# One level of Strassen's product for all projections of x in a hybrid encoder block

## The chip, the core and the metric

The kernel runs on one core of a Trainium2 chip. The metric is the device time of one execution in microseconds (us); the median of three runs counts. The core has five engines that run side by side: TensorE (PE in the profile; PEld is its weight load), VectorE (DVE), ScalarE (ACT), GpSimd (POOL) and SyncE (SP), whose queue issues most DMAs.

## The reference

All arrays are float32. One layer over 1024 tokens of 1024 channels:

```python
h = rmsnorm(x, norm_mix_g)                      # (1, 1024, 1024)
z = h @ w_in                                    # 1024 -> 4*512 + 3*512 + 8 + 512 + 3*1024 columns
(hq, hf, hi, hg, fq, fk, fv, ff, mq, gate_logits) = split(z)
y_a = hgrn2(hq, hf, hi, hg)                     # gated recurrence, 4 heads, 128x128 state
y_b = fox(fq, fk, fv, ff)                       # forgetting attention, 8 heads of 64, causal
y_c = memory(mq, rmsnorm(mem) @ mem_kv_w)       # cross attention into 256 tokens, 4 heads of 128
gates = sigmoid(gate_logits)                    # three gates per channel
merged = gates[0]*(y_a @ w_br_hgrn) + gates[1]*(y_b @ w_br_fox) + gates[2]*(y_c @ w_br_mem)
x = x + merged @ w_out
x = x + conv_glu(rmsnorm(x, norm_ffn_g))        # up to 2*2816, causal conv of width 3, gelu, down
```

The projection `h @ w_in` is the part that the change touches: the columns `hq, hf, hg, mq` and the gates are wanted channel-major (channels on partitions), `hi, fq, fk, fv` token-major, and `ff` gives eight forget logits per token.

## The kernel before

Float32 products are made from three passes: each operand is split into a high part of reduced precision (`h`, a cast on ACT or POOL) and the rest (`l`, a subtraction on DVE), and `mm3` (L109 to L111) issues h·h, h·l and l·h into one PSUM bank. `split` is at L115 (cast on ACT), L119 (on POOL) and L123 (subtraction). A block of the contraction is 128 channels; a bank holds 512 float32 columns. There are eight banks in four tags: `pp` (three), `lg` (two), `tr` (two) and `po` (one).

Start-up. x arrives as eight slices `xk` of 128 channels by 1024 tokens, memory as `mt`, its weights as `wkv`. The list `SEQ` orders the work by hand: memory keys and values (`kv_chunk`), and as slices of x land, their split into `uh`, `ul` (L269, L270), and two gate chunks (`gate_step`) are multiplied slice by slice. x is split unnormalized; the norm's factor per token (`rt`, from rows of x that are loaded a second time, and `rx`, the same spread over partitions by a DMA through DRAM) is applied to the products.

Projections of x. A channel-major chunk (`cm_chunk`) is 128 columns of the weight against 1024 tokens: 2 halves x 8 blocks x 3 matmuls of 512 columns. A token-major piece (`token_major`) is 256 weight columns for 8 blocks of tokens: 8 x 8 x 3 matmuls of 256 columns.

Mixers. `fox_values` (token-major fv and the forget logits) run first, then fox runs over four pairs of heads. `weave` interleaves the program of a mixer with that of fill: `fox_attn` with the next pair's `fox_proj` and gate chunks (`gates_early`, results stored to DRAM as `gd`), the last pair with HGRN2's values, `hgrn_mix` with the next head's `hgrn_prep`, `mem_attn` with `mem_prep` and gates. `ahead` gives the mixers a head start of 300 places in priority; within that, a scheduler orders each engine's instructions when the kernel is built. Outputs of HGRN2 and memory stay in SBUF (`ya`, `yc`), those of fox go through DRAM and are loaded back as `yb` while the memory mixer runs.

Merge. `gates` goes over 24 chunks (three branches of eight): branch product (`br_chunk`), gate, sum. One gate chunk is still made there, the others come from DRAM. Then the output product, and the feed-forward part, which already uses one level of Strassen's product: `unit` makes four blocks of output from seven products of 12 matmuls, on seven families of operand blocks kept in SBUF (B11, T1, T2, B22, T3, B21, T4), with sums of weight blocks made on DVE. At its start `second_norm` makes the norm from column sums (L1030) and `spread` (L288).

Of the kernel before, what the change touches and what calls it, by code (L numbers as in the profile page):

```python
# [8 lines left out]
F32 = mybir.dt.float32  # L9
# [5 lines left out]
P = 128  # L15
# [14 lines left out]
NGF = [0, 3, 1, 2, 0, 5, 2, 0]  # L30
NG = [1, 1, 0, 3, 0, 0, 0, 3]
NPRE = 2 + sum(NG) + sum(NGF)
FOX_STEPS, HGRN_STEPS, MEM_STEPS = 28, 24, 7
FOX_LATE, MEM_LATE = 0.2, 0.3
AHEAD = 300
SEQ = ("k0 k1 k2 k3 x0 x1 g0 x2 mr g1 k4 s0 s1 x3 s2 k5 x4 mn mk s3 k6 x5 s4 k7 mv x6 s5 x7 xn s6 s7").split()
# [29 lines left out]
def tile_block(ctx: ExitStack, tc: tile.TileContext, xT, memT, x_rows, mem_rows, vec, fbias, mats, hmask, w_cm, w_hi, w_fqk, w_fv,  # L66
# [5 lines left out]
    wp = tc.alloc_tile_pool(name="wp", bufs=2, side="left")  # L72
# [22 lines left out]

# [29 lines left out]
    def rstd_small(out, ss, n):  # L125
        w = ss.shape[1]
        V.tensor_scalar(out, ss, 1.0 / n, EPS, ALU.mult, ALU.add)
        G.tensor_tensor(out, out, mhalf[:, :w], ALU.pow)

    wsplit = [S, V]  # L130

    def raw_weights(src, n):
        raw = wp.tile([P, 4 * 264], F32, tag="raw", name="raw", bufs=2)
        SP.dma_start(raw[:, :n], src)
        return raw

    def weights(src, shape, raw=None, hl=None, parts=1):

        n = shape[0] * shape[1]
        if raw is None:  # L140
            raw = raw_weights(src, n)
        if hl is None:
            hl = [wp.tile([P, 4 * 264], F32R, tag=t, name=t, bufs=3) for t in ("wh", "wl")]
        for i in range(parts):
            sl = slice(i * n // parts, (i + 1) * n // parts)
            split(wsplit[0], hl[0][:, sl], hl[1][:, sl], raw[:, sl], wsplit[1])
        return [t[:, :n].rearrange("p (a b) -> p a b", a=shape[0]) for t in hl]

    def cm_chunk(src, nk, rh, rl, by_channel=False):


        wh, wl = weights(src, (nk, P))
        if by_channel:
            pss = [ps_proj(), ps_proj()]
            for k in range(nk):
                for n, ps in enumerate(pss):
                    sl = slice(n * HB, (n + 1) * HB)
                    mm3(ps, wh[:, k, :], wl[:, k, :], rh[k][:, sl], rl[k][:, sl], k == 0, k == nk - 1)
            yield from enumerate(pss)
            return  # L160
        for n in range(2):
            ps = ps_proj()
            sl = slice(n * HB, (n + 1) * HB)
            for k in range(nk):
                mm3(ps, wh[:, k, :], wl[:, k, :], rh[k][:, sl], rl[k][:, sl], k == 0, k == nk - 1)
            yield n, ps

# [3 lines left out]
    pu = tc.alloc_tile_pool(name="pu", bufs=1, side="left")  # L171

    def both_parts(name):

        t = [[pu.tile([P, T], F32R, tag=f"u{p}{k}", name=f"{name}{p}{k}") for p in "hl"] for k in range(KC)]
        return [a for a, _ in t], [b for _, b in t]

    uh, ul = both_parts("u")
    rx = pu.tile([P, T], F32, tag="rx", name="rx")
    rt = pu.tile([P, 8], F32, tag="rt", name="rt")  # L180

    kvd = tc.dram_tile([P, 2, T], F32, name="kvd")

    p0 = tc.alloc_tile_pool(name="p0", bufs=1, side="right", reuse_waits="tile")
    mt = p0.tile([P, KC, NM], F32, tag="mt", name="mt")
    xk = [p0.tile([P, T], F32, tag="xk", name=f"xk{k}", bufs=5) for k in range(KC)]
    def row_tile(name):
        return p0.tile([P, 2 * HB], F32, tag="wkv", name=name, bufs=6)  # L190

    wkv = [row_tile(f"wkv{q}") for q in range(4)]
    mem_row = [row_tile(f"mr{i}") for i in range(2)]
    wkv += [row_tile(f"wkv{q}") for q in range(4, 8)]
    x_row = [row_tile(f"xr{i}") for i in range(6)]
    x_row[2:2] = [p0.tile([P, T], F32, tag="xk", name=f"xr{i}", bufs=5) for i in (6, 7)]
    SP.dma_start(cv, vec)
    for q in range(4):
        w = 2 if q else 1
        for i in range(2 // w):  # L200
            sl, ws = slice(2 * q + i, 2 * q + i + w), slice(i * HB, (i + w) * HB)
            SP.dma_start(mt[:, sl, :], memT[:, sl, :])
            SP.dma_start(wkv[q][:, ws], w_mkv[q][:, ws])
    SP.dma_start(ones, mats[:, P:2 * P])
    rgw = []
    for what in SEQ:
        if what[0] == "x" and what != "xn":
            k = int(what[1])
            SP.dma_start(xk[k], xT[:, k, :])
        elif what == "mr":  # L210
            for i in range(2):
                SP.dma_start(mem_row[i], mem_rows[i])
        elif what[0] == "g":
            br, j = order[int(what[1])]
            rgw.append(raw_weights(w_cm[16 + 8 * br + j], KC * P))
        elif what in ("k4", "k5", "k6", "k7"):
            q = int(what[1])
            SP.dma_start(wkv[q], w_mkv[q])
    SP.dma_start(ident, mats[:, 0:P])
    for i in range(8):  # L220
        last_row = SP.dma_start(x_row[i], x_rows[i])
# [1177 lines left out]
```

## Time and profile before

| | |
|---|---|
| median of 3 runs | 1768.04 us (1767.48 to 1768.28) |
| span of the profiled execution, first to last instruction | 1765.2 us, so 2.8 us less than the median |
| PE busy | 1749.7 us (99%), 9153 matmul records |
| DVE, ACT, POOL busy | 1127.0, 742.8, 330.9 us |
| mean granted TensorE clock | 0.999 |
| DMA | 213.71 MB, mean 121 GB/s |

The profile is of one execution. A plain float32 matmul leaves two records, one of reduced precision leaves one. Matmuls are pipelined: a record's duration is longer than the distance to the next, so busy time counts their union. A row of a group has: line, engine, operation, output<-inputs, shapes and count, then busy time, mean ns of one, and the engine's idle time before them with what ended it. A row of a window has its start and end, its length, then busy time and count for PE, PEld, DVE, ACT and POOL, the granted clock, the DMA engines' share and GB/s. A row of the timeline has the start, the duration, engine, line, operation and tiles, and the idle time before. A row of the chain has the start, the duration and what ran.

### The profile page before, as it was taken

How to read it: one execution, taken by the hardware profiler on the slowest of the kernel's cores; microseconds unless marked ns; L12 is line 12 of the kernel's file. 1: busy time of each engine (PE TensorE's matmuls, PEld its weight loads, DVE VectorE, ACT ScalarE, POOL GpSimd, SP SyncE). 2: the span in 40 equal slices, each digit the busy share in tenths (PEclk: the TensorE clock that was granted, in tenths of full speed). 3: DMA queues.
4: the chain of work that ended last, by engine and by line, in shares of the span. 5: the costliest groups of instructions: out<-in, count | busy, mean ns of one | idle time of the engine just before them, and what ended most of it. 6: DMA issues, size and time to landing. Idle time of an engine off the chain costs nothing.

```text
span 1765.2 us, 24344 instructions
## 1 busy us (share of the span) xinstructions
PE 1749.7 (99%) x9153; PEld 1483.6 (84%) x9153; DVE 1127.0 (64%) x2065; ACT 742.8 (42%) x1237; POOL 330.9 (19%) x416
## 2 busy tenths in 40 slices
PE   8999999999999999999999999999999999999999
PEld 6999899889988888888888888788888888778887
DVE  6236665665567787734446665787777877775654
ACT  8345555554544354324522143643433443433332
POOL 0015233343224333323100000111111111100000
PEclk9999999999999999999999999999999999999999
DMA  9311121221111111130144442465544444394682
GB/s 365 142 61 65 63 74 49 101 76 52 61 63 37 42 43 37 52 128 19 66 143 132 143 180 83 133 186 160 147 141 151 125 126 143 132 380 148 221 289 84
DMA packets 77014, 213.71 MB, mean 121 GB/s; under 512 B 8912, under 2 KB 11736, under 8 KB 76768
## 3 DMA queue, kind: packets, MB, share of 16 engines
q1 hardware_dynamic: 62016, 159.19, 25.8%
q0 software_dynamic: 14880, 52.96, 10.5%
q8 instruction: 72, 1.18, 0.3%
q14 instruction: 46, 0.38, 0.1%
HBM read 174.07 MB, written 61.12 MB: 133 GB/s over the span
## 4 chain that ended last, share of the span: by engine, by line
PE 98%; DMA 1%; ACT 0%; SPq 0%; DVE 0%; issue 0%; DVEq 0%
PE pp L110 22%; PE pp L111 22%; PE pp L109 22%; PE lg L110 4%; PE lg L111 4%; PE lg L109 4%; PE tr L109 2%; PE tr L110 2%; PE tr L111 2%; PE lg L700 2%; PE po L567 1%; PE lg L526 1%; PE po L566 1%; PE lg L525 1%; PE po L111 1%; PE po L110 1%
## 5 line engine op out<-in xcount | busy, mean ns | idle before, releaser
L111 PE MATMUL pp<-uh,wl 128*128 128x512 f32 x608 | 243.6, 401 | 0.0
L110 PE MATMUL pp<-ul,wh 128*128 128x512 f32 x608 | 243.2, 400 | 0.0
L109 PE MATMUL pp<-uh,wh 128*128 128x512 f32 x608 | 241.7, 397 | 0.0
L110 PE MATMUL pp<-wl,uh 128*128 128x256 f32 (+1 forms) x512 | 145.0, 284 | 0.0
L111 PE MATMUL pp<-wh,ul 128*128 128x256 f32 (+1 forms) x512 | 144.5, 283 | 0.0
L109 PE MATMUL pp<-wh,uh 128*128 128x256 f32 (+1 forms) x512 | 143.7, 283 | 0.0
L115 ACT CAST wh<-raw 128x1024 fp32r<-128x1024 f32 (+2 forms) x80 | 73.0, 914 | 158.7 <-PE pp L110 124.9
L109 PEld LDWEIGHTS pp<-uh,wh 128*128 128x128 f32 x608 | 115.3, 190 | 23.3
L110 PEld LDWEIGHTS pp<-ul,wh 128*128 128x128 f32 x608 | 114.5, 188 | 22.9
L111 PEld LDWEIGHTS pp<-uh,wl 128*128 128x128 f32 x608 | 114.4, 188 | 22.5
L123 DVE TENSOR_TENSOR wl<-raw,wh 128x1024 fp32r<-128x1024 f32 (+2 forms) x87 | 93.8, 1080 | 34.1 <-ACT wh L115 23.8
L1078 POOL DMA_DIRECT2D rw<-in_w_up x44 | 24.2, 557 | 466.5 <-DVE wl L123 413.3
L115 ACT CAST wh<-s 128x512 fp32r<-128x512 f32 x85 | 51.9, 619 | 124.7 <-PE pp L110 64.7
L110 PEld LDWEIGHTS pp<-wl,uh 128*128 128x128 f32 x512 | 96.4, 188 | 0.8
L111 PEld LDWEIGHTS pp<-wh,ul 128*128 128x128 f32 x512 | 96.5, 189 | 0.6
L109 PEld LDWEIGHTS pp<-wh,uh 128*128 128x128 f32 x512 | 96.2, 189 | 0.8
L115 ACT CAST dwh<-wr 128x1024 fp32r<-128x1024 f32 (+1 forms) x42 | 41.1, 980 | 121.4 <-PE tr L110 41.7
L115 ACT CAST wh<-rw 128x512 fp32r<-128x512 f32 x65 | 40.1, 620 | 86.7 <-PE pp L110 46.7
L123 DVE TENSOR_TENSOR dwl<-wr,dwh 128x1024 fp32r<-128x1024 f32 (+1 forms) x42 | 47.6, 1132 | 35.5 <-ACT dwh L115 35.1
L681 POOL TENSOR_TENSOR X<-X,kt 128x256 f32<-128x256 f32 x48 | 48.3, 1012 | 110.2 <-ACT X L680 110.1
L543 POOL TENSOR_SCALAR pt<-pt,st 128x128 f32<-128x128 f32 (+3 forms) x64 | 57.0, 891 | 63.3 <-DVE st L542 51.4
L541 ACT ACTIVATE pt<-pt,st 128x128 f32<-128x128 f32 (+3 forms) x64 | 49.7, 777 | 33.9 <-DVE st L538 29.4
(422 smaller groups left out, 4797.3 us busy)
## 6 DMA issues: line engine op xcount, KB each, us to landing
rw<-in_w_up POOLq DMA_DIRECT2D x44, 512.0 KB, 4.6
raw<-in_w_cm SPq DMA_DIRECT2D x40, 512.0 KB, 3.5
sd<-in_w_dn POOLq DMA_DIRECT2D x30, 512.0 KB, 6.0
br<-yd SPq DMA_DIRECT2D x30, 512.0 KB, 5.0
gd<-gt SPq DMA_DIRECT2D x46, 256.0 KB, 2.0
gt<-gd SPq DMA_DIRECT2D x46, 256.0 KB, 2.7
yd<-fc SPq DMA_DIRECT2D x44, 256.0 KB, 2.6
wr<-sd SPq DMA_DIRECT2D x20, 512.0 KB, 4.7
```

The source lines that it names most:

```text
L109: PE.matmul(ps, lh, rh, start=first, stop=False, skip_group_check=more)
L110: PE.matmul(ps, lh, rl, start=False, stop=False, skip_group_check=more)
L111: PE.matmul(ps, ll, rh, start=False, stop=last, skip_group_check=more)
L115: S.copy(out, in_)
L123: return (sub or V).tensor_sub(l, src, h.bitcast(F32))
L525: PE.matmul(ps[:, :w], qa[i][:, tsl], kh[i][:, s0:s0 + w], start=True, stop=False)
L526: fox_sets[p][3] = PE.matmul(ps[:, :w], qa[i][:, tsl], kl[i][:, s0:s0 + w], start=False, stop=True)
L541: S.activation(pt[:, :ns], pt[:, :ns], AF.Exp, bias=st[:, 2:3], accum_out=st[:, 3:4])
L543: G.tensor_scalar(pt[:, :ns], pt[:, :ns], st[:, 3:4], 0.0, ALU.mult, ALU.add)
L681: G.tensor_mul(Xk, Xk, Kv[:, :, 0, :])
L700: PE.matmul(o[:, b * 64:(b + 1) * 64], X[:, b * P:(b + 1) * P], Xq[:, b * bpb:(b + 1) * bpb, :], start=True, stop=True)
L1078: late["raw"] = G.dma_start(raw[:, 2 * i:2 * i + 2, :], src[:, 2 * i:2 * i + 2, :])
```

## The change

All projections of x are made by one level of Strassen's product. With x in quarters (two halves of the channels by two halves of the tokens) and the weight in quarters, seven products of half size replace eight.

- Families. x is normalized first: squares are summed over the slices as they land (`x_square`), the factor comes from column sums, a power on POOL and `spread`; each quarter is then multiplied by gain and factor (`normed`), combined and split into seven families of 4 x 128 channels by 512 tokens, which stay in SBUF until the mixers end. The rows of x are not loaded, and no gate chunk is made at start-up. The forget logits come from 16 plain float32 matmuls (`forget_logits`), ordered behind the spread.
- A dense token-major stage: four units (`tm_unit`) of seven products of 48 matmuls of 256 columns: hi, two units of fk and fq, fv. Weights come as four loads of 512 KB, sums of weight blocks are made on POOL. The results go to DRAM (`hid`, `kqd`, `vhd`, `ffd`, `negFd`), keys and queries normed, transposed and split beforehand.
- Channel-major projections come in pairs of chunks: twenty units (`cm_unit`) of seven products of 12 matmuls, in the order of `UNITS`. They are the only fill of the mixers, through `islice(fill, n)`. Results go to DRAM (`hgd`, `mqd`, `gd`).
- The mixers load all inputs from DRAM, and store their outputs there (`yd3`). `fox_prep`, `hgrn_prep` and the values kept in SBUF (`Vf`) are gone. `load_y` brings a branch's 2 MB back ahead of its eight chunks, into one buffer; the first time right after the memory mixer.
- POOL's scratch for DMAs is set to 4096 bytes (`dynamic_dma_scratch_size`).

The core of the diff:

```diff
-NGF = [0, 3, 1, 2, 0, 5, 2, 0]
-NG = [1, 1, 0, 3, 0, 0, 0, 3]
+FOX_FILL = [0, 6, 6, 6, 6, 6, 6, 6]
+HGRN_FILL = [21, 21, 21, 21]
+MEM_FILL = [5, 4, 3, 2]
+UNITS = [[("f", 0), ("q", 0)], [("g", 0), ("f", 1)], [("q", 1), ("g", 1)], [("f", 2), ("q", 2)],
+         [("g", 2), ("f", 3)], [("q", 3), ("g", 3)], [("mq", 0), ("mq", 1)], [("mq", 2), ("mq", 3)]]
+UNITS += [[("gt", i), ("gt", i + 1)] for i in range(0, 24, 2)]
...
+    def x_square(k):
+        if k == 0:
+            S.activation(acc, xk[0], AF.Square)
+            return
+        sq = xp.tile([P, T], F32, tag="sq", name="sq")
+        S.activation(sq, xk[k], AF.Square)
+        V.tensor_add(acc, acc, sq)
...
+    def forget_logits():
+        for k in range(KC):
+            for n in range(2):
+                PE.matmul(pairs[1][n][:8, :], wff[:, k, :], xk[k][:, n * HB:(n + 1) * HB], start=k == 0, stop=k == KC - 1)
...
+    for tb in range(8):
+        PE.matmul(ps[:, tb:tb + 1], acc[:, tb * P:(tb + 1) * P], ones[:, 0:1], start=True, stop=True)
+    x_rstd = rstd_small(rt, ps[:, :8], D)
+    spreads = spread(rx, rt)
+    mem_values()
+    with tc.issue_after(spreads.ins):
+        forget_logits()
...
+    for k in range(4):
+        family_block("B11", k, normed(0, 0, k))
+    for k in range(4):
+        normed(1, 1, k, G)
+    for k in range(4):
+        family_block("B21", k, normed(1, 0, k))
...
+    for k in range(4):
+        tt = temps[:, 2 * (k % 2):2 * (k % 2) + 2, :]
+        V.tensor_sub(tt[:, 0, :], quarter(0, 0, k), normed(0, 1, k))
+        V.scalar_tensor_tensor(out=tt[:, 1, :], in0=tt[:, 0, :], scalar=-1.0, in1=quarter(1, 1, k),
+                               op0=ALU.mult, op1=ALU.subtract)
+        family_block("T2", k, tt[:, 1, :])
+        family_block("T1", k, tt[:, 0, :])
+        V.scalar_tensor_tensor(out=quarter(0, 0, k), in0=tt[:, 1, :], scalar=-1.0, in1=quarter(1, 0, k),
+                               op0=ALU.mult, op1=ALU.subtract)
...
+    def tm_sum(a, b):
+        t = rp.tile([P, T], F32, tag="ws", name="ws", bufs=2)
+        with tc.issue_after(x_rstd.ins):
+            G.tensor_add(t, a, b)
+        return t
...
+    def cm_unit(u, puts):
...
+        a11, a12, a21, a22 = raw
+        o1, o6 = u_operand(a11), u_operand(a12)
+        s1 = u_sum(a21, a22)
+        s2 = u_sum(s1, a11)
+        u_product(x, o1, "B11", True)
+        e1 = u_snap(x)
+        yield
+        u_product(z, o6, "B21", True)
+        put(0, 0, z, e1)
+        o3 = u_operand(s2)
+        yield
+        u_product(x, o3, "T2", False)
+        e2 = u_snap(x)
+        o2 = u_operand(s1)
+        s4 = u_sum(s2, a12)
+        yield
+        u_product(y, o2, "T1", True)
+        e5 = u_snap(y)
+        o5 = u_operand(u_sum(a11, a21))
+        yield
+        u_product(x, o5, "T3", False)
+        put(1, 1, x, e5)
+        o4 = u_operand(s4)
+        yield
+        u_product(y, o4, "B22", False)
+        put(0, 1, y, e2)
+        o7 = u_operand(a22)
+        yield
+        u_product(x, o7, "T4", False)
+        put(1, 0, x, None)
+        yield
...
+    for h in range(8):
+        weave((ahead(fox_attn(h), AHEAD), FOX_STEPS), (islice(fill, FOX_FILL[h]), FOX_FILL[h]))
+    pf.release()
...
+    for h in range(4):
+        weave((ahead(hgrn_mix(h), AHEAD), HGRN_STEPS), (islice(fill, HGRN_FILL[h]), HGRN_FILL[h]))
...
+    run_all(fill)
+    ur.release()
+    pfam.release()
```

`u_operand` is a `split`, `u_sum` an addition on POOL, `u_snap` a copy of a bank on ACT, and `u_product` four blocks of `mm3` against a family.

More of the change, by code (lines that the diff above doesn't have):

```diff
@@ L149, in cm_chunk @@
[L149 to L166, printed above, removed]
@@ L169, in tile_block @@
-    order = [(br, j) for br in (1, 0, 2) for j in range(8)]
[L171 to L196, printed above, removed]
@@ L222, in tile_block @@
+    SP.dma_start(ident, mats[:, 0:P])
+    load_x(3)
+    for q in range(4, 8):
+        load_kv(q)
+        load_x(q)
+    SP.dma_start(wff, w_ff)
     G.memset(mhalf, -0.5)
@@ new lines, in spread @@
+    def spread(r, rcol):
+        for n in range(2):
+            ps = ps_tr()
+            for b in range(4):
+                last = PE.matmul(ps[:, b * P:(b + 1) * P], rcol[:, 4 * n + b:4 * n + b + 1].to_broadcast([P, P]), ident,
+                                 start=True, stop=True)
+            S.copy(r[:, n * HB:(n + 1) * HB], ps)
+        return last
+    for k in range(KC):
+        mem_chunk(k)
+    for q in range(4):
+        kv_chunk(q)
+        if q < 3:
+            x_square(q)
+    mem_norm()
```

838 lines of the change are left out of this document (454 added, 384 removed).

## The prediction

> **What bounds the kernel now.** I read the page first: span, engine shares, slices, chain.
>
> ```profile
> span 1765.2 us, 24344 instructions
> PE 1749.7 (99%) x9153; PEld 1483.6 (84%) x9153; DVE 1127.0 (64%) x2065; ACT 742.8 (42%) x1237; POOL 330.9 (19%) x416
> ...
> PE   8999999999999999999999999999999999999999
> ...
> PEclk9999999999999999999999999999999999999999
> ...
> PE 98%; DMA 1%; ACT 0%; SPq 0%; DVE 0%; issue 0%; DVEq 0%
> ```
>
> TensorE's matmuls are the kernel: the chain that ended last is 98% PE, and only the first slice shows a gap. A matmul taken away is time saved; a gap put in is time lost. Next the stages, from the busy times in windows: start-up, a stretch of it, the token-major values, forgetting attention ("fox"), HGRN2, memory, two moments at the start of the feed-forward part, and its steady state.
>
> ```profile
> core 0: us, PE busy (x) PEld busy (x) DVE busy (x) ACT busy (x) POOL busy (x), PEclk, DMA share, GB/s
> 0.00:58.00 58.00, 51.22 (x223) 40.90 (x224) 32.93 (x49) 42.96 (x63) 6.51 (x10) 1.00 0.88 330
> 16.00:36.00 20.00, 19.47 (x83) 15.13 (x82) 16.40 (x19) 18.16 (x22) 3.27 (x2) 1.00 1.03 408
> 58.00:132.00 74.00, 74.00 (x627) 73.83 (x626) 22.84 (x32) 28.42 (x47) 7.81 (x9) 1.00 0.23 81
> 132.00:480.00 348.00, 348.00 (x2272) 315.45 (x2272) 212.74 (x644) 179.25 (x349) 129.38 (x167) 1.00 0.21 69
> 520.00:775.00 255.00, 255.00 (x1441) 216.76 (x1439) 184.73 (x365) 96.84 (x174) 83.14 (x76) 1.00 0.12 44
> 775.00:875.00 100.00, 100.00 (x549) 85.31 (x548) 48.37 (x105) 45.46 (x112) 27.59 (x41) 1.00 0.21 72
> 1124.00:1127.00 3.00, 0.40 (x2) 0.33 (x2) 0.41 (x1) 3.00 (x7) 0.62 (x2) 0.97 0.96 374
> 1127.00:1130.20 3.20, 3.20 (x15) 3.07 (x14) 3.20 (x6) 1.70 (x4) 0.81 (x2) 0.50 0.08 32
> 1160.00:1500.00 340.00, 340.00 (x1471) 275.90 (x1470) 264.31 (x394) 138.40 (x211) 46.43 (x75) 1.00 0.49 144
> ```
>
> The mixers run without a gap, because projection matmuls fill every wait. The listed mean of a matmul (0.4 us for 512 columns) holds its latency; its price is the pace. The feed-forward row gives 340/1471 = 0.231 us for 512 columns, the token-major row 74/627 = 0.118 us for 256.
>
> **Matmuls removed.** Before, 40 channel chunks of x take 48 matmuls of 512 columns each, 1920; eight token-major pieces take 8 x 8 x 3, 1536 of 256. After, 20 units of seven products of 12 make 1680, and four token-major units of seven products of 48 make 1344. So 240 x 0.231 = 55.4 us and 192 x 0.118 = 22.7 us go: 78.1 us.
>
> **Matmuls added.** The forget logits become 16 plain float32 matmuls of 512 columns, instead of eight extra columns in a token-major piece. The norm of x comes from column sums (8 matmuls of one column) and a spread (8 of 128) instead of a DMA round trip. The nearest rows are an HGRN product in float32, the eight transposes of the old forget path, and the second norm, which makes the same steps:
>
> ```profile
> 530.30 0.95 PE tr L725 x8
> ...
> 107.03 0.87 PE tr L437 x8
> ```
>
> ```profile
> 1118.81 0.95 PE L1030 MATMUL po<-ones,r 128*128 128x1 f32 x8
> 1122.41 1.66 POOL L128 TENSOR_TENSOR rt<-rt,mhalf 128x8 f32<-128x8 f32 x1
> 1126.61 0.62 PE L109 MATMUL pp<-T3h,wh 128*128 128x512 f32 x1 [2.60 <-ACT wh L115]
> 1127.46 3.28 PE L288 MATMUL tr<-ident,rt 128*128 128x128 f32 x16
> 1129.41 0.58 ACT L290 COPY r<-tr 128x512 f32<-128x512 f32 x1 [1.29 <-PE tr L288]
> ```
>
> L725's eight records are four float32 matmuls of 128 columns, 0.24 us each, so 512 columns cost 0.95 and sixteen 15.2 us. The ends are 3.7 us (16 x 0.231, were it one pass) and 30.4 (half clock); L725 is the same arithmetic, so I take it. The spread ran at half clock, so 1.6 us at full; column sums 2 x 0.95; the transposes return 0.9. Added: 15.2 + 1.6 + 1.9 - 0.9 = 17.8. Matmul work alone falls by 60.3 us. Memory keys and values, attention and recurrence, and all from the branch products on keep their matmuls; the key transposes only move from the fox loop into the dense stage.
>
> **Start-up.** Before, gate products ran chunk by chunk as x landed. Now no product of x can start until all of x has landed, been squared, summed, spread and multiplied in.
>
> ```profile
> 35.47 1.04 ACT L350 ACTIVATE xr<-xr 128x1024 f32<-128x1024 f32 x1
> ...
> 36.51 1.14 ACT L269 ACTIVATE uh<-xk,cv 128x1024 fp32r<-128x1024 f32 x1
> ```
>
> ```profile
> L123 DVE TENSOR_TENSOR wl<-s,wh 128x512 fp32r<-128x512 f32 x85 | 58.0, 683 | 4.9 <-ACT wh L115 4.9
> L1183 DVE TENSOR_TENSOR fc<-fc,r 128x1024 f32<-128x1024 f32 x22 | 26.8, 1220 | 3.1 <-ACT fc L1182 3.1
> ```
>
> The last slice of x is cast at 36.5 us. Three loads of 512 KB ahead of it go (two gate weights, one row block): 1.57 MB at 408 GB/s is 3.9 us, so it lands near 32.6. Then square 1.0, add 1.2, sums 1.9, power 1.7, spread 1.6 to 3.3, copy 0.6: the scale row stands near 41.6. By the spread's end, near 41, PE has had the memory's 96 matmuls (22.2 us) and 3.5 of sums and spread since 5.8: 9.5 idle, against 1.0 now (58 - 51.2 - 5.8): +8.5. The forget logits cover PE to 56, the B11 and B21 products (48 x 0.118 = 5.7 each) to 67.6. T2 needs some 41 DVE steps of 0.683 after the scale row and a weight split of 1.2, near 70.8: a wait of 3 (0 to 8). Start-up: +11.5 (5 to 18). A later token-major unit has 336 x 0.118 = 40 us of PE over some 28 of DVE (7 splits and 8 norm steps of 1.2, 14 half steps of 0.7); I cost those at nothing, as feed-forward units run with DVE at 264/340 and no gap.
>
> **Hand-overs.** Everything now goes to the mixers through DRAM.
>
> ```profile
> nf<-negFd SPq DMA_DIRECT2D x8, 512.0 KB, 3.8
> ...
> yb<-ybd SPq DMA_DIRECT2D x1, 2048.0 KB, 11.5
> ```
>
> From the dense stage to fox, buffers are reused: loads (3.8), cast and split (0.6 + 0.7) of the first fill unit wait for the dense stage's last tiles, with little but the last product (5.7) over them. I take 4 us (0 to 10). At the end of the memory mixer, the 2 MB of fox output are loaded into space that the last fill unit frees: 5.1 us at 408 GB/s to 11.5 by the row, plus cast and split of 1.0 + 1.2, under the tail of the last memory head. I take 7 (0 to 14). Before, that place was covered by a gate chunk and the output was resident.
>
> **Fox with less fill.** The fox stage loses its key, query and gate products (576 x 0.118 + 13 x 48 x 0.231 = 212 us) and some 30 of HGRN values, and gains 42 fill steps of 12 (116 us): PE 348 - 242 + 116 = 222. DVE keeps
>
> ```profile
> L123 DVE TENSOR_TENSOR pl<-tr,ph 128x512 fp32r<-128x512 f32 (+1 forms) x80 | 49.6, 631 | 17.3 <-ACT ph L115 16.9
> L531 DVE CUSTOM_DVE_ANT_0 pt<-lg,nf 128x512 f32<-128x512 f32 (+2 forms) x80 | 41.5, 527 | 29.5 <-PE tr L554 14.7 <-PE lg L526 13.9
> L531 DVE CUSTOM_DVE_ANT_0 pt<-lg,nfm 128x128 f32<-128x128 f32 x64 | 18.3, 285 | 12.1 <-POOL nfm L520 3.8 <-PE tr L557 2.9 <-PE tr L554 2.4
> L571 DVE TENSOR_TENSOR yp<-po,yp 64x256 f32<-64x256 f32 x32 | 13.2, 412 | 5.7 <-ACT yp L570 5.5 <-ACT ph L115 0.2
> L538 DVE TENSOR_SCALAR st<-st 128x1 f32<-128x1 f32 x56 | 11.5, 206 | 0.7
> L542 DVE RECIPROCAL st<-st 128x1 f32<-128x1 f32 x64 | 10.3, 161 | 32.2 <-ACT pt L541 32.0
> ```
>
> 144 us, plus six units of some 12.7 steps at 0.683, 52: 196 of 222, 88%. That is tighter than the feed-forward part's 78%, so 3 us (0 to 20). In HGRN2 and memory ACT and DVE have more room (184.73 of 255, 48.37 of 100, now with fill that needs less of them): nothing. ACT's extra work there (a logarithm per half head, so more table loads) and the extra DMAs on SP's queue lie beside PE; SP's are stores and prefetches at a DMA share of 0.12 to 0.23. Were that cover gone, a head would pay the 3.8 us above (the third rival). The smaller scratch for POOL's DMAs I cost at nothing: feed-forward loads have POOL busy 46 of 340 us.
>
> **Clock.** After the 2.6 us gap above, the clock was 0.50 for the 3.2 us row. So three gaps (T2, fox, branches) cost 1.6 each beside themselves: 4.8. [...]
>
> **Sum.** -60.3 + 11.5 + 4 + 3 + 7 + 4.8 = -30.0. The profiled span is 1765.2, the median of the runs 1768.04, 2.8 around it, which stays. 1735.2 + 2.8 = 1738.
>
> **Rivals.** First, the scheduler interleaves well enough that only the late start (8.5) stays: -60.3 + 8.5 gives 1716; the mixers' gapless windows speak for it, the new hand-overs against. 20% (1705 to 1718).
>
> Second, POOL's sums hold up DVE. Each unit adds four POOL additions of 512.
>
> ```profile
> L681 POOL TENSOR_TENSOR X<-X,kt 128x256 f32<-128x256 f32 x48 | 48.3, 1012 | 110.2 <-ACT X L680 110.1
> L682 DVE TENSOR_TENSOR X<-X,hq 128x256 f32<-128x256 f32 x48 | 29.6, 628 | 6.5 <-ACT X L680 6.4
> L678 DVE TENSOR_TENSOR X<-Gt 128x256 f32<-128x256 f32 x48 | 21.4, 449 | 8.7 <-PE lg L691 5.4 <-PE lg L700 3.4
> ```
>
> At 1.01 us per 256 a sum takes 2.0. If DVE stood still for each, fox would need 196 + 48 = 244 against PE's 222, 22 where I took 3: 1757. HGRN2 would still fit: of its 255 us, 14 chunks of projection (155 us of PE, some 48 of DVE) go and 12 units (233 and 82) come, so 333 of PE over 219 + 96 of DVE. L682, which starts beside L681, takes 0.18 us longer than L678, a fifth of POOL's time: then fox needs 206 and nothing changes. 5%. [...]
>
> Third, slower: mixer loads arrive late, as SP's queue holds them behind stores that wait. There are 20 hand-overs (eight fox heads, eight HGRN2 halves, four memory heads) at up to 3.8 us of the row above, 1738 to 1814; the kernel is slower than before from (30 + 3.5)/20 = 1.7 us each. Against it: the eight loads of that kind before cost PE nothing. 10%. That the product count does not fall is excluded by the code.
>
> **How the numbers follow.** My forecast has 62%, with its own range 1718 to 1758 from the bounds of start-up, hand-overs and fox; 3% lie around no change. Below 1709 and above 1764 I leave some tenth each. A change under 0.2% could hardly be measured here: faster means below 1764.5, slower above 1771.6. Faster 0.62 + 0.20 + 0.05 = 0.87; same 0.03; slower 0.10.
>
> **What would show it.** PE records near 8,780 (9153 - 432 + 64 - 9) and busy time near 1690; the forget logits near 15 us; a PE gap of 8 to 10 us before 45 us, one of 3 before the T2 products; gaps of 4 and 7 at the two transitions, each with a PEclk dip; DVE under 95% in fox. I am wrong if PE idles inside the fox or HGRN stages (second and third rivals: the waits name POOL's sums or a DMA), or if the transitions are seamless (first).

## The result and the profile after

The changed kernel takes 1787.8 us (median of 4 runs, 1786.6 to 1788.9) against 1768.16 for the kernel before: ratio 1.0114 (95% interval 1.0100 to 1.0129), slower by about 20 us. The forecast was 1738. The times below are medians too, and each ratio is to the kernel before, run beside it.

The head of the page of the changed kernel:

```profile
span 1786.5 us, 24626 instructions
PE 1709.1 (96%) x8776; PEld 1434.1 (80%) x8776; DVE 1259.9 (71%) x2214; ACT 836.6 (47%) x1405; POOL 463.0 (26%) x467
...
PE   7899959999999999999799999999999999999999
...
PEclk9999979999999999999799999999999999999999
...
PE 84%; DVE 5%; DMA 4%; POOL 2%; ACT 2%; issue 1%; SPq 1%; DVEq 0%; POOLq 0%; ACTq 0%
```

PE lost 377 records and 40.6 us of busy time, but the span grew by 21.3. Idle PE (span less busy) went from 15.5 to 77.4 us. Of the chain that ended last, 98% was PE, and now it is 84%. Busy time by stages: start-up, the families, the dense stage, the hand-over to fox, fox, HGRN2, memory, the rest.

```profile
0.00:58.00 58.00, 45.36 (x161) 28.82 (x162) 38.05 (x67) 36.77 (x53) 12.04 (x13) 0.91 0.68 249
58.00:100.00 42.00, 33.66 (x211) 29.32 (x209) 39.69 (x51) 21.22 (x36) 18.11 (x7) 0.88 0.17 52
100.00:244.00 144.00, 144.00 (x1209) 144.00 (x1207) 90.88 (x94) 62.93 (x83) 53.52 (x19) 1.00 0.34 122
244.00:274.00 30.00, 6.59 (x23) 4.47 (x22) 5.43 (x24) 5.53 (x12) 4.47 (x8) 0.60 0.92 247
274.00:605.00 331.00, 327.99 (x1767) 278.98 (x1766) 229.61 (x665) 192.43 (x395) 165.86 (x180) 1.00 0.43 129
605.00:852.00 247.00, 239.08 (x1377) 203.17 (x1376) 218.40 (x403) 144.56 (x265) 118.82 (x100) 1.00 0.35 119
852.00:922.00 70.00, 56.36 (x312) 47.78 (x311) 39.42 (x82) 46.13 (x107) 24.42 (x37) 0.85 0.37 138
922.00:1786.50 864.50, 856.01 (x3733) 697.59 (x3731) 598.47 (x833) 327.05 (x457) 65.75 (x105) 1.00 0.54 168
```

The idle time stands in four places: start-up and families (12.6 + 8.3), the hand-over (23.4), HGRN2 (7.9), memory (13.6). (Fox has 3.0, and the 8.5 of the rest were there before, as 8.7.) In and behind the holes the granted clock was 0.50 in these stretches:

```profile
23.90:30.70 6.80, 5.47 (x12) 3.89 (x13) 5.94 (x8) 6.11 (x8) 1.82 (x1) 0.50 1.03 408
44.40:47.80 3.40, 3.40 (x16) 2.77 (x15) 0.00 (x0) 0.99 (x2) 3.32 (x2) 0.50 0.00 0
71.70:75.10 3.40, 3.40 (x19) 3.40 (x18) 3.40 (x7) 1.35 (x2) 0.00 (x0) 0.50 0.07 10
92.20:99.00 6.80, 5.98 (x29) 5.94 (x29) 5.49 (x8) 3.75 (x7) 1.91 (x1) 0.50 0.57 207
249.20:273.10 23.90, 5.42 (x14) 3.60 (x15) 3.84 (x21) 2.73 (x8) 3.57 (x8) 0.50 0.94 254
867.00:887.50 20.50, 15.47 (x70) 15.09 (x70) 9.50 (x18) 11.44 (x22) 6.02 (x8) 0.50 0.51 196
```

The PE column sums to 39.1 us at half clock. I count half of it, 19.6, as loss, an estimate from the clock of 0.50 (matmuls of 512 columns start 0.43 us apart from 27.05 to 30.04 us, and 0.23 from 31.3 on). Without it PE was busy for 1709.1 - 19.6 = 1689.5 us, against some 1749.7 - 1.7 = 1748.0 before (3.4 us at half clock): by this estimate the work itself fell by 58.5.

**The hand-over from the dense stage to fox.** SP's queue, one wait, and PE around the hole:

```profile
237.81 5.94 SPq L543 DMA_DIRECT2D vhd<-vo  x3
243.84 1.21 SPq L682 DMA_DIRECT2D kh<-kqd  x2
...
254.13 2.20 SPq L687 DMA_DIRECT2D vhl<-vhd  x2
256.63 5.78 SPq L543 DMA_DIRECT2D vhd<-vo  x1
262.45 0.43 SPq L676 DMA_DIRECT2D mskf<-in_mats  x1
262.93 1.75 SPq L633 DMA_DIRECT2D ur<-in_w_cm  x3
```

```profile
POOL nfm L702 <- DMA mskf<-in_mats: 51.7, 1, 51.7
```

```profile
243.99 0.28 PE L110 MATMUL pp<-wh,T4l 128*128 128x256 f32 x1
255.38 0.77 PE L707 MATMUL lg<-kh,qa 128*128 128x128 f32 x2 [11.11 <-DMA qa<-kqd]
```

Each load form is issued twice (x2): those of heads 0 and 1 alternate, both ahead of the causal mask (262.45), which the first head needs, and of the first fill weights (262.93). The value stores (L543) in this queue wait for DVE's splits, 19.9 us in five waits between 230 and 265.

**The hand-over to memory.** The longest wait of the memory stage, 8.38 of its 13.6 us, is at its start:

```profile
860.17 0.33 SPq L894 DMA_DIRECT2D yd<-hz  x1
861.29 0.33 SPq L1023 DMA_DIRECT2D yr<-yd  x1
...
862.67 1.24 SPq L921 DMA_DIRECT2D mqr<-mqd  x2
...
871.94 0.58 PE L108 MATMUL lg<-mkh,mqh 128*128 128x256 f32 x1 [8.38 <-ACT mqh L114]
```

The first head's queries are loaded behind HGRN2's last store and a load of another branch's output; they are cast at 870.84, 8.2 us after the issue, and the DMA share is 0.95 to 1.00 from 864 to 870. No fill is left to cover the wait. The hole that was forecast, at the end of the memory mixer, did not come: the first 2 MB of a branch's output were already on their way at 847, beside the last HGRN2 head, and after 915 us PE never waits for more than 0.4 us before the merge goes on.

**Where the fill went.** The records that have a fill operand (`uh`, then `ul`), in the hand-over and fox, HGRN2, memory:

```profile
244.00:605.00 361.00, 213.71 (x657) 0.97 0.48 139
605.00:852.00 247.00, 149.21 (x464) 1.00 0.35 119
852.00:922.00 70.00, 0.00 (x0) 0.85 0.37 138
```

```profile
244.00:605.00 361.00, 128.83 (x328) 0.97 0.48 139
605.00:852.00 247.00, 91.63 (x232) 1.00 0.35 119
```

657 + 328 of 1680 fill matmuls, 82 of 140 steps, ran by the end of fox, where `FOX_FILL` names 42. In the memory mixer none was left (the `ul` row there is 0 too). `islice` fixes where a step is traced, not where it runs: the scheduler pulled 40 steps ahead into fox.

**DVE beside POOL.** In the families DVE (first) and POOL (second):

```profile
85.58 0.67 DVE L136 TENSOR_TENSOR e<-po,e 128x512 f32<-128x512 f32 x1
86.17 1.68 DVE L390 SCALAR_TENSOR_TENSOR xk<-T4h,xk 128x512 f32<-128x512 f32 x1
87.78 2.82 DVE L122 TENSOR_TENSOR T3l<-xk,T3h 128x512 fp32r<-128x512 f32 x1
90.52 0.68 DVE L122 TENSOR_TENSOR T2l<-T4h,T2h 128x512 fp32r<-128x512 f32 x1
```

```profile
81.57 5.73 POOL L423 TENSOR_TENSOR ws<-ws,raw 128x1024 f32<-128x1024 f32 x1 [13.90 <-issue]
87.38 2.67 POOL L423 TENSOR_TENSOR ws<-raw 128x1024 f32<-128x1024 f32 x1
```

A DVE step of 0.67 us takes 2.82 while a POOL sum of 2.67 stands beside it. The POOL sum before takes 5.73, while most of DVE's steps stay at 0.67; with DVE idle, at 43.89 us, a sum took 2.33. T2's split, for which PE waits here (3.4 us), comes behind T3's.

### The profile page after: what moved, and what is told of

It reads as the page before. It is cut to its first block, busy times and chain, and to the rows that moved or that the text cites. A ratio compares the mean times of both kernels' runs of the same rounds, so it can differ in the third digit from the quotient of the medians.

```text
span 1786.5 us, 24626 instructions
## 1 busy us (share of the span) xinstructions
PE 1709.1 (96%) x8776; PEld 1434.1 (80%) x8776; DVE 1259.9 (71%) x2214; ACT 836.6 (47%) x1405; POOL 463.0 (26%) x467
## 4 chain that ended last, share of the span: by engine, by line
PE 84%; DVE 5%; DMA 4%; POOL 2%; ACT 2%; issue 1%; SPq 1%; DVEq 0%; POOLq 0%; ACTq 0%
PE pp L110 17%; PE pp L108 17%; PE pp L109 17%; PE lg L108 5%; PE lg L110 5%; PE lg L109 5%; PE tr L108 2%; PE tr L110 2%; PE tr L109 2%; PE lg L840 1%; PE po L109 1%; PE po L110 1%; PE po L108 1%; PE po L749 1%; PE po L748 1%
## 5 line engine op out<-in xcount | busy, mean ns | idle before, releaser
L122 DVE TENSOR_TENSOR ul<-us,uh 128x512 fp32r<-128x512 f32 x80 | 74.7, 936 | 16.5 <-ACT uh L114 16.0
L568 POOL TENSOR_TENSOR us<-ur 128x512 f32<-128x512 f32 x40 | 57.4, 1434 | 60.0 <-DVE ul L122 23.3
L725 POOL TENSOR_SCALAR pt<-pt,st 128x128 f32<-128x128 f32 (+3 forms) x64 | 52.8, 827 | 38.2 <-DVE st L724 34.5
L114 ACT CAST uh<-us 128x512 fp32r<-128x512 f32 x80 | 49.4, 617 | 27.8 <-PE pp L109 26.4
L122 DVE TENSOR_TENSOR wl<-s,wh 128x512 fp32r<-128x512 f32 x85 | 58.1, 684 | 4.8 <-ACT wh L114 4.8
L122 DVE TENSOR_TENSOR wl<-raw,wh 128x512 fp32r<-128x512 f32 (+1 forms) x45 | 45.8, 1020 | 19.6 <-ACT wh L114 18.8
L568 POOL TENSOR_TENSOR us<-us,ur 128x512 f32<-128x512 f32 x40 | 54.7, 1368 | 18.8 <-DVE ul L122 9.2
L122 DVE TENSOR_TENSOR pl<-tr,ph 128x512 fp32r<-128x512 f32 (+1 forms) x80 | 49.4, 630 | 11.5 <-ACT ph L114 11.4
L108 PE MATMUL pp<-yh,wh 128*128 128x512 f32 x144 | 55.2, 390 | 1.7 <-ACT yh L114 1.7
L109 PE MATMUL pp<-yl,wh 128*128 128x512 f32 x144 | 56.2, 391 | 0.3 <-DVE yl L122 0.3
L707 PE MATMUL lg<-kh,qa 128*128 128x512 f32 (+2 forms) x96 | 35.7, 374 | 21.5 <-DMA qa<-kqd 11.1
L110 PE MATMUL pp<-yh,wl 128*128 128x512 f32 x144 | 56.1, 389 | 0.0
```

The source lines that it names most:

```text
L108: PE.matmul(ps, lh, rh, start=first, stop=False, skip_group_check=more)
L109: PE.matmul(ps, lh, rl, start=False, stop=False, skip_group_check=more)
L110: PE.matmul(ps, ll, rh, start=False, stop=last, skip_group_check=more)
L114: S.copy(out, in_)
L122: return (sub or V).tensor_sub(l, src, h.bitcast(F32))
L568: G.tensor_add(t, a, b)
```

## Experiments

The letters are explained in each expectation. The main theories: Q, the order of SP's queue makes the hole at the hand-over to fox; F or S, fill spent too early makes the idle time of the mixers. Their rival C: the mixers run at the pace of their own chains (the steps of a head that wait for one another), and fill does not change that. Other runs ask what DVE and POOL cost. From the rationing run with the queue order on, most runs build on the one before.

**Queue order.** Mask loaded in start-up; a head's loads held behind the first output store of the head before; one fill step traced ahead of head 0.

```diff
+        with tc.issue_after(stored.pop().ins) if stored else nullcontext():
+            kh, kl, qa, vhl, nf = fox_load(h)
...
+    next(fill)
     for h in range(8):
```

> The mask is loaded at start-up, head h+1's loads of keys, queries and values are queued behind head h's first output store, and the first step of fill is traced ahead of the first fox head. Theory Q (the 24 us hole after the dense stage is the order in SP's queue: two heads' loads stand ahead of the mask and of the first fill weights): the hole shrinks from 24 to about 10 us and the time falls by 12 to 18 us, to 1770 to 1776. Rival D (the hole is the trip of keys and values through DRAM itself): first fox matmul and first DVE step of fox stay where they were, change under 3 us.

1775.4 us, ratio 1.0052 (1.0035 to 1.0070): 12 us less, as theory Q has it. The run makes three edits at once and does not tell how much each of them is worth. The stretch around the hole of this kernel has 10.4 us of idle PE, not 23.4:

```profile
235.00:265.00 30.00, 19.60 (x121) 17.00 (x121) 12.49 (x45) 11.23 (x23) 7.41 (x13) 0.77 0.71 229
```

**Fill kept for the memory mixer.** The products of the last two units held behind HGRN2's last matmul.

```diff
+        with tc.issue_after(held[-1].ins) if held else nullcontext():
```

> The matmuls of the units traced in the memory mixer (14 steps, the last two units) may not be issued before the last matmul of HGRN2's last head. Theory F (the fill was used up early: the fox and HGRN2 stages are bound by PE, so what is taken out of them shortens them, and the memory stage gets cover): PE idle and half clock between 845 and 925 us go, time falls by 18 to 28 us, to 1760 to 1770. Rival C (fox and HGRN2 run at the pace of their own chains, and fill was pulled in because PE had nothing else): the 39 us taken out of them leave holes there, time 1783 to 1790.

1801.4 us, ratio 1.0197 (1.0177 to 1.0216): slower by 14, and above the range of either theory. The 8.4 us wait at the start of the memory mixer is gone, but PE idled where the fill was taken from (14 us between 740 and 800, at a clock of 0.82), and HGRN2's last scan started only 11 us earlier (775.5, not 786.6). A hole that is filled at one place opened at another.

**All fill first.**

```diff
+    run_all(fill)
     for h in range(8):
```

> All twenty units are traced ahead of the mixers, which then run with no fill beside them. The pace of a fox head alone tells what binds it. Theory F: 17 to 30 us a head against 41 with fill, HGRN2 under 45 us a head against 62. Rival C: fox 36 us a head or more, HGRN2 55 or more. The time itself is 150 to 350 us longer in both.

1906.9 us (one run). The edit did not do for fox what was expected: the scheduler still ran fill beside seven of its eight heads, the last fill matmul at 730.4 us. So only the last fox head, HGRN2 and memory are shown alone. The rows are the end of fox and HGRN2:

```profile
725.00:785.00 60.00, 42.67 (x219) 33.33 (x217) 32.98 (x116) 30.07 (x58) 15.98 (x25) 0.82 0.42 135
785.00:935.00 150.00, 98.74 (x517) 86.72 (x518) 115.60 (x251) 68.92 (x119) 57.63 (x57) 0.68 0.19 62
```

HGRN2's scans, two a head, come every 17 to 25 us: 40 to 46 us a head while PE has time to spare, but at a mean clock of 0.68, so this is no floor at full clock. Theory F said under 45, rival C 55 or more. The last fox head, with no fill beside it, took 21.5 us from its first exponential to its last, at a clock of 0.92; in the runs below every later head, with fill beside it, took 28.5 us or more.

**Forget logits.** Seven eighths of their contraction are left out.

```diff
-        for k in range(KC):
+        for k in range(1):
```

> Leaves out seven eighths of the contraction of the forget logits (14 of 16 float32 matmuls). If they lie in the shadow of the families, as predicted: 0 to 4 us faster, and a hole stands where they were. If they are on the path: 11 to 13 us faster.

1790.2 us, ratio 1.0130 (1.0113 to 1.0147): no gain. A hole of 11.8 us stands in their place. They lay in the shadow of the families, as predicted.

**Rationing.** Fill of head h's weave held behind the last matmul of the head before.

```diff
+            if tp == 3:
+                held.append(last_fox)
...
+            if n == 1:
+                held.append(last_hg)
```

> Each fill product of head h's weave is ordered behind the last matmul of the mixer head before it, so that fill can no longer be spent ahead of its place: 41 of 140 steps stand before the end of fox instead of 82, 65 in HGRN2, 34 in the memory mixer. A step is 12 x 0.231 = 2.77 us, a fox head has 12.4 us of matmuls of its own. Theory S (fill spent early is what stretched fox; the fox chain itself needs under 30 us a head): heads of 28 to 31 us instead of 41, fox 230 to 250 us instead of 331, the memory mixer covered at full clock, kernel 1750 to 1770. Rival C (the fox chain itself needs 35 us or more a head, as the 34.5 us of the head behind the fill showed): holes of 5 to 10 us in every fox head, fox 290 us or more at a low clock, memory longer by its 94 us of fill, kernel 1785 to 1830.

1836.7 us, ratio 1.0391 (1.0373 to 1.0408): theory S falls, and rival C's holes came, 2 to 6 us in six fox heads (the time is above C's range, too). Fox had 37 us of idle PE in 271, at a clock of 0.93. The hold also gives a head with no fill at all: the two rows go from the first exponential of head 0 to that of head 1, and from there to head 2. In the first no fill matmul ran, in the second 60.

```profile
267.10:292.40 25.30, 17.37 (x79) 12.68 (x79) 17.11 (x68) 13.09 (x31) 15.85 (x21) 0.77 0.51 135
292.40:330.10 37.70, 29.54 (x155) 24.76 (x154) 22.84 (x76) 17.51 (x38) 14.82 (x19) 0.91 0.39 102
```

The head with fill kept PE busy for 12.2 us more and took 12.4 us longer; PE was idle for about 8 us in both. So in this pair five steps of fill did not go into the waits of the head, they lengthened it. That is neither S nor C: a head alone is faster than C says. It is one pair, and head 0 has no head before it.

**Rationing with the queue order.**

```diff
+FOX_FILL = [4, 6, 6, 6, 6, 6, 6, 6]
+    next(fill)
```

> The rationing of the run before together with the queue change (mask and the loads of later heads no longer stand ahead of the first fill weights on SP's queue), one fill step before head 0 and four beside it: 46 of 140 steps before the end of fox. Theory S: another 12 us less than with rationing alone, 1738 to 1758, faster than the kernel before. Rival C: the queue change alone is kept, so 12 us less than a rationing that loses, 1773 to 1818.

1806.6 us, ratio 1.0211 (1.0191 to 1.0232): in rival C's range, not in S's.

**Eight steps a head.**

```diff
+FOX_FILL = [4, 8, 8, 8, 8, 8, 8, 8]
+HGRN_FILL = [15, 16, 16, 16]
+MEM_FILL = [5, 4, 4, 3]
```

> As the queue change with rationing, but eight fill steps a fox head instead of six (59 of 140 before the end of fox, 53 in HGRN2, 28 in the memory mixer). Theory S (heads can go at under 30 us): slower than six a head by 0 to 10, 1745 to 1768, since the PE work of fox is only moved. Theory C (heads need about 35): 8 x 2.77 + 12.4 = 34.6 fills a head exactly, holes vanish, and this one is faster than six a head by 10 to 40 us, 1745 to 1775.

1787.7 us, ratio 1.0111 (1.0086 to 1.0135): 19 less than with six, the direction that theory C has; both theories had put the time lower, at 1775 or less. With these runs the pace of a fox head can be read from the starts of the heads' first exponentials (last six heads):

| fill steps a head | PE work, 12.4 + 2.77 a step | measured pace |
|---|---|---|
| 6 | 29.0 us | 34.2 us |
| 8 | 34.6 | 35.5 |
| 9 (a later run) | 37.3 | 38.2 |
| 10.3 (changed kernel) | 40.9 | 41.4 |

With six steps a head takes 5 us more than its PE work; from eight steps on the two are within 1 us, and PE sets the pace. The 34 us are not the chain of a head alone, which took 25.3 us without fill in the rationing run (its first head, at a clock of 0.77). What lengthens it, the fill's place in PE's order or its casts, splits and sums on ACT, DVE and POOL, no run here separates. In the changed kernel fox is PE-bound (PE busy for 327.99 of 331 us), and the fill spent there lacks in memory.

**Weight sums on DVE.**

```diff
-        G.tensor_add(t, a, b)
+        V.tensor_add(t, a, b)
```

> The four weight sums of each fill unit (80 additions of 128x512) run on DVE instead of POOL. Theory L (POOL's sums hold DVE up: the fill subtractions last 936 ns beside them where those of the feed-forward part last 684): the subtractions fall to about 700 ns, 80 x 0.23 = 18 us, against 80 additions x 0.70 = 56 us more on DVE, which has 100 us of room in fox and 30 in HGRN2; time within 6 us of 1788 and no hole goes. Rival D (DVE is what sets the pace of fox and HGRN2): 56 us more DVE work between 274 and 852 lengthen these stages by 10 to 40 us, kernel 1798 to 1828.

1802.7 us, ratio 1.0193 (1.0178 to 1.0208): in the range of rival D (more work on DVE lengthens the mixers). The subtractions behind the sums fell to a median of 686 ns from 720, but the whole is 15 us slower. POOL's sums cost DVE something and are still better where they are.

**More fill beside the first HGRN2 head.**

```diff
+HGRN_FILL = [24, 14, 14, 13]
```

> As the run with eight steps a fox head, but the first HGRN2 head gets 24 fill steps (the others 14, 14, 13) instead of 15 and 16s. There fill was used up at 560 us, and 560 to 600 had 13 us of idle PE and some 14 us lost to a clock of 0.63 to 0.77. Theory H (holes stand where the fill of that place is used up, whatever was spent before): the stretch is covered, 1787.7 falls by 12 to 25, to 1763 to 1776. Rival P (the hole comes from POOL, where a multiply of the recurrence stands behind a fill sum that waits for DVE): it stays, 1782 to 1792.

1779.2 us, ratio 1.0073 (1.0058 to 1.0088): 8.5 less, under the 12 that theory H expected, but more than rival P leaves; idle time of 560 to 600 fell from 13 to 8 us, and DVE was busy for 38 of these 40 us.

**Value stores on POOL's queue.**

```diff
-            SP.dma_start(vhd[c][:, 4 * n + 2 * b:4 * n + 2 * b + 2, :, :], vo.bitcast(F32))
+            G.dma_start(vhd[c][:, 4 * n + 2 * b:4 * n + 2 * b + 2, :, :], vo.bitcast(F32))
```

> As the run before, and the four value stores of the last dense units are issued by POOL, so that head 0's loads no longer stand behind them on SP's queue (the last of these stores was issued at 240.9 us, the loads at 241.3 to 244.5; PE was idle from 241.4 for 7.4 us). Theory Q (SP's order sets the hole): the loads start up to 10 us earlier, the hole shrinks to 0 to 3 us with the half-speed stretch behind it, 6 to 11 us less than the run before. Rival B (the loads wait for the dense stage's buffers): less than 2 us.

1774.6 us, ratio 1.0050 (1.0035 to 1.0065): 4.6 less, between theory Q and rival B. Fox's first exponential came at 249.1, not 256.2.

**Families in another traced order.**

```diff
-        family_block("T2", k, tt[:, 1, :])
-        family_block("T1", k, tt[:, 0, :])
...
+        family_block("T2", k, quarter(0, 0, k))
+    for k in range(4):
+        family_block("T1", k, temps[:, k, :])
```

> As the run before, and the families are built in another order: all four blocks of T2 first (four DVE steps a block instead of six), T1's splits behind them, the combination for T4 only in front of T4's own splits. PE waited 2.8 us at 66.4, 3.5 us at 86.9 and some 3 us in smaller gaps there, with 10 us at half clock behind them, while DVE was busy for 39.7 of 42 us. Theory D (DVE's order of work sets these gaps): 4 to 10 us less than the run before. Rival E (DVE's total work up to T4 sets the time, in any order): within 2 us.

1778.2 us, ratio 1.0066 (1.0049 to 1.0082): 3.6 more than the run before, so nothing gained. Theory D falls for this order; rival E (DVE's total work) had said within 2 us.

**Nine steps a head.**

```diff
+FOX_FILL = [6, 9, 9, 9, 9, 9, 9, 9]
+HGRN_FILL = [24, 12, 10, 10]
```

> As the run with the value stores on POOL, but nine fill steps a fox head (six beside head 0) and fewer beside the later HGRN2 heads (24, 12, 10, 10). With eight, PE was busy 243 of 255 us in fox (265 to 520) and fully busy in HGRN2 from 600 on: a head needs 36 us and its PE work is 12.4 + 8 x 2.77 = 34.6; with nine 37.3. Theory H (idle PE goes where fill is added, as long as the chain keeps its pace): fox stays within 6 us of its length, 8 to 10 us of its idle time go, 1774.6 becomes 1763 to 1769. Rival C (each fill step lengthens the fox chain too, as PE takes instructions in order): fox grows by 8 x 2.77 = 22 us, nothing is gained, 1772 to 1780.

1772.7 us, ratio 1.0041 (1.0025 to 1.0056). The gain over the run with the value stores on POOL, 1.9, lies within the spread of both; the time is in rival C's range, and the pace of a fox head went from 36.2 to 38.2 us. This is the lowest median of all versions (two later ones are within 2 us of it), still 7 us slower than the kernel before. Its windows around fox and HGRN2:

```profile
235.00:265.00 30.00, 22.01 (x119) 18.54 (x119) 15.00 (x50) 13.49 (x29) 14.33 (x20) 0.77 0.57 195
265.00:545.00 280.00, 274.12 (x1483) 232.78 (x1481) 199.64 (x611) 166.63 (x342) 142.63 (x160) 0.99 0.49 141
545.00:600.00 55.00, 49.27 (x245) 39.58 (x243) 38.65 (x60) 34.30 (x56) 19.63 (x18) 0.97 0.48 159
600.00:800.00 200.00, 196.05 (x1148) 169.08 (x1148) 183.22 (x344) 114.31 (x215) 103.30 (x89) 0.98 0.29 99
```

**First unit without weight sums** (one raw block is used in place of each sum).

```diff
+        total = tm_sum if u else lambda a, b: a
+        s1 = total(a21, a22)
```

> The changed kernel, with the four POOL weight sums of the first dense unit left out (the first raw block is used in their place). Theory L (POOL's work beside DVE's slows DVE in the start-up: B11's subtractions take 949 ns and the norm steps 915 beside it, 676 in T1 and T2): from 45 to 100 us DVE's 39.7 busy us shrink by 4 to 8, and the gaps before T2's products with them; 1781 to 1786. Rival D (DVE's own work is what the products wait for, sums or not): within 2 us of 1788.

1788.6 us, ratio 1.0130 (1.0113 to 1.0146): as rival D has it (DVE's own work is what the products wait for). B21's subtractions fell from 945 to 674 ns, T3's from 1212 to 672, and no time was gained: idle PE fell from 8.3 to 6.6 us between 58 and 100 and rose from 12.6 to 14.8 ahead of it, and DVE was still busy for 39.95 of the 42 us.

**Head 1's loads earlier.**

Here `ex` is head 0's first exponential.

```diff
+                if h == 0 and tb == 0:
+                    stored.append(ex)
```

> As the run with nine steps, and head 1's loads are ordered behind head 0's first exponential instead of its first output store. With eight steps PE waited 1.4 and 2.2 us for head 1's keys at 271 to 275 us. Theory Q (load order): 2 to 5 us less than with nine steps alone, 1759 to 1766. Rival B: these loads delay the fill weights behind them again, as in the changed kernel: 2 to 6 us more.

1777.0 us, ratio 1.0059 (1.0044 to 1.0074): 4.3 more than with nine steps, as rival B has it; the two intervals still overlap.

**Families in an order held by waits.**

T2's blocks are held behind B21's last subtraction (`built`), and T1, then T3, B22 and T4 behind T2's (`built_t2`).

```diff
+        with tc.issue_after(built.ins):
...
+        with tc.issue_after(built_t2.ins):
```

> As the run with nine steps, and DVE's work on the families is put in the order of the products by holds: T2's blocks behind B21's last subtraction, T1, T3, B22, T4 and the adds of B21's result behind T2's last. In the run with the value stores on POOL, splits of T3 and B22 ran before T2's third block (T2's subtraction at 90.6 us), and single DVE operations there lasted 1.7 and 2.8 us beside POOL's sums. Theory O (the scheduler's order of DVE's work sets the gaps of 2.8 and 3.6 us before T2's matmuls; reordering the trace alone left it free to mix them): the two gaps and the half clock behind them go, 6 to 12 us less than with nine steps, 1761 to 1767, and T3's products start before 95 us. Rival L (POOL's sums hold DVE up wherever it works): gaps move to T3 or T4, within 3 us of 1772.7.

1774.0 us, ratio 1.0035 (1.0022 to 1.0047): as rival L has it. Of the gaps of 2.6 and 3.4 us before T2's matmuls one of 1.2 was left, and gaps of 2.0, 1.0, 0.5 and 1.1 came before matmuls of T3 and B22. Four additions for T3 (0.68 each in the changed kernel) take 5.69 us beside POOL's sums:

```profile
82.23 5.69 DVE L404 TENSOR_TENSOR xk<-xk,xk 128x512 f32<-128x512 f32 x4
87.85 2.48 DVE L122 TENSOR_TENSOR B22l<-xk,B22h 128x512 fp32r<-128x512 f32 x4
```

```profile
75.22 8.15 POOL L431 TENSOR_TENSOR ws<-ws,raw 128x1024 f32<-128x1024 f32 x1 [8.08 <-issue]
83.45 2.72 POOL L431 TENSOR_TENSOR ws<-raw 128x1024 f32<-128x1024 f32 x1
```

**First fill step above the mixer.**

```diff
+    with tc.high_priority(2000):
+        next(fill)
```

> As the run with nine steps, with the first fill step traced at a priority above the mixer, so that its two weight loads stand ahead of head 0's bias row and values on SP's queue, and eight steps beside head 0. With nine steps PE was idle for 7.2 us at 242 us and the stretch 235 to 265 had 8 us idle at a clock of 0.77. Theory W (the hole is a lack of matmuls to run there, since fill cannot start until its weights have landed and been split): the first fill matmul starts by 248 instead of 254, hole and half clock shrink by 4 to 9 us, 1764 to 1769. Rival B (loads, casts and splits of fill delay head 0's own chain by as much): within 3 us of 1772.7.

1774.6 us, ratio 1.0043 (1.0029 to 1.0057): as rival B has it. The hole shrank from 7.0 to 3.0 us, but head 0's first exponential came at 254.2 instead of 250.0, and the rest followed.

## Why the prediction was wrong

The work was right: 8776 records forecast as 8780, and 58.5 us less matmul work forecast as 60.3. What failed is the idle time and the half clock around it: the steps that took start-up, hand-overs and mixers as covered, or nearly so. By place, extra over the kernel before, with half clock counted where it fell:

| | forecast | measured |
|---|---|---|
| matmul work | -60.3 | -58.5 |
| start-up and families | +11.5, +1.6 clock | +14.1, +9.1 clock |
| dense stage to fox | +4, +1.6 clock | +23.4, +2.7 clock |
| fox | +3 | +3.0 |
| HGRN2 | 0 | +7.9 |
| memory and its end | +7, +1.6 clock | +13.6, +7.7 clock |
| the rest | 0 | -1.8 |
| sum | -30.0 | +21.2 |

The excess of 51 us has four parts. The -1.8 of the rest is luck: the kernel before lost 1.7 us to half clock at the start of its feed-forward part, and the changed kernel has a gap of nearly the same length there (2.54 us, not 2.60) without it.

- **Dense stage to fox (20).** "I take 4 us (0 to 10)": I counted one load, cast and split. I did not count what SP's queue holds ahead of them: stores that wait for DVE's splits, then two heads' loads. That is the third rival's mechanism, at one hand-over instead of twenty; the queue run shows 12 us of it, and the value stores on POOL's queue 4.6 more.
- **Memory (13).** "The mixers run without a gap, because projection matmuls fill every wait" was carried over to the kernel after, which assumes the fill where the lists put it. The trace shows it spent 40 steps early. With none left, the late load of the first head's queries stood bare (8.4 us, and 7.7 of half clock in its wake); the queue order is the third rival's again. "I take 7 (0 to 14)" was for another hole, the load behind the memory mixer, which did not come; that 13.6 lies inside its range is luck. Keeping fill for this place did not win the time: it moved the idle time to fox and HGRN2. The assumption that failed there is that less fill still goes into a mixer's waits: in one pair of heads of the rationing run five steps lengthened a fox head by 12.4 us for 12.2 us more of busy PE, and the idle time stayed. The trace of before could not show this, as its fill was ample. Why fill lengthens a head is open.
- **Start-up (10).** Of the 10, 7.5 are half clock and 2.6 idle time. Instead of one gap of 8 to 10 us before 45 us, two came, of 3.6 and 2.0. I took one gap before T2 (3 us), and one half-clock stretch for it; four stretches came, 9.1 us, two of them behind the gaps before 45 us, which I had costed without any. "T2 needs some 41 DVE steps of 0.683": beside POOL some steps take 1.68 to 2.82 us, and DVE is busy for 39.69 of 42 us. Neither leaving out the first unit's sums nor another order of DVE's work gained time; what is left as the likely bound is DVE's total work up to T4, which no run here took away. So this cause stays open.
- **HGRN2 (8).** I cost it at nothing from its averages (DVE 184.73 of 255). After, DVE is at 218.40 of 247, and at 38 of 40 us in one stretch of the run with more fill beside the first head. That DVE makes these waits is likely, not shown: PE's waits in the stage name ACT (5.0 us) more than DVE (3.0), none of them above 2 us.

The second rival, POOL holding up DVE, shows in single steps (2.82 us for one of 0.67 beside a POOL sum), but moving the fill's sums to DVE or leaving out the first unit's gained nothing. Fox's own term (+3.0 for 3) was right by luck: it was worked out for 42 steps of fill, and 82 ran. With 41 to 46 steps fox had 37 us (rationing) and 20 us (with the queue order, 260 to 500) of idle PE.

Not settled: why about 34 us remain between the best version (span 1769.1) and the forecast span of 1735.2. Its idle PE is 57.4 us, spread over start-up (21.8), the hand-over (8.0), fox (5.9), the start of HGRN2 (5.7), later mixers (7.5) and the rest (8.5), and its mean clock is 0.986. Most attempts at one place gave back part of their gain at the next.

## What to carry over

When a change removes work that also served as cover, don't take it that what is left still fills the waits. Read from a run how long a stage takes with none of that work beside it, and again with the amount that will be left: here one fox head took 25.3 us with none and the next 37.7 with five steps, with the same idle time. And check in the trace where the fill ran, not where it was traced. At each hand-over write out the queue of loads and stores in issue order: the price here (PE waited 11.11 us for head 0's queries in fox and 8.38 for those of memory) was set by what stood ahead of the first load that was needed, and by what fill was left to cover it. Count half clock as a possible cost of each hole, not once for each stage: here it came behind gaps of 2.00 and 2.63 us, and not behind one of 2.54.

## What the runs showed of the hardware

- Gaps of 2 to 3 us were followed by half clock at some places and not at others. The first row is at 44 us in the changed kernel, where the clock is 0.50 from 44.4 on for 3.4 us. The others are behind a gap of 2.54 us at 1145.6 us, where it stays at 1.00:

```profile
43.96 0.83 PE L320 MATMUL tr<-ident,rt 128*128 128x128 f32 x4 [2.00 <-POOL rt L127]
```

```profile
1145.60:1148.20 2.60, 0.09 (x1) 0.09 (x1) 0.11 (x1) 2.60 (x6) 0.00 (x0) 1.00 0.50 180
1148.20:1151.60 3.40, 3.40 (x23) 3.12 (x24) 3.40 (x6) 2.60 (x5) 0.71 (x2) 1.00 0.00 0
```

  The kernel before had its half clock at that second place (0.50 for 3.4 us from 1126.8, behind a gap of 2.60), so the same step of two kernels can have the loss or not. Ahead of the first gap stand sixteen records of one-column sums, 1.84 us from 40.12 on. Half clock also came behind a gap of 2.63 us at 67.4 (0.50 from 71.7 to 75.1). And between 867 and 887.5 PE was busy for 15.47 of 20.5 us at a clock of 0.50 throughout; 6.8 us of that are sums of one column.
- DVE and POOL operations took longer beside each other: 2.82 us for a DVE step of 0.67, 5.73 us (8.15 in the run with the order held by waits) for a POOL sum that took 2.33 and 2.34 with DVE idle, from 43.89 us on. The DVE step of 2.82 us ended 0.55 us after the POOL sum beside it. Over many DVE steps in a row it was POOL that took longer: seven steps of 0.67 us ran within the 5.73.
- Of the build, not the chip: `islice` and program order don't bind a scheduler that fills free places: 82 steps ran where 42 were traced.
